# Low weight parts of two stages: ScalarE and an accumulating transfer in place of GpSimd's subtraction

## The chip, the cores and the metric

One core of a Trainium2 chip runs the whole program. The metric is device time in microseconds (us). Five engines run side by side, each with its own queue of instructions in a fixed order: TensorE (PE; its weight loads are PEld), VectorE (DVE), ScalarE (ACT), GpSimd (POOL) and SyncE (SP, which only starts transfers). Transfers that SP starts go through one DMA queue, those that GpSimd starts through another.

## The reference

Two layers over 512 tokens of 1024 columns. What matters here is the first half of a layer: the input projection, the gated channels (u, v) and the output projection `w_o`. All is float32.

```python
h = x @ w_in[i]
q, k, v, qi, ki, wi, u, vs = jnp.split(h, split_points, axis=-1)
a_out = dsa_attention(q, k, v, qi, ki, wi)               # 8 heads, top-k keys
b_out = spatial_gating(gelu(u), gelu(vs), sgu_w[i], ...) # u * (W_s LN(v) + b)
mix = jnp.concatenate([a_out, b_out], axis=-1) @ w_o[i]
x = layer_norm(ALPHA * x + mix, ln1_g[i], ln1_b[i])
```

Behind it stand the feed-forward part and a second layer norm, which the change doesn't touch.

## The kernel before

**Products in three parts.** Each float32 operand is split into a rounded high part h and the rest l = w - h, and a product is three matmuls, h·h, h·l and l·h (`mm3`, L473). For weights `split` (L457) does that: ScalarE casts 1024 columns of the loaded page `raw` into `wh` (L467), and an engine that the caller names subtracts, wl = raw - wh (`low`, L364). The caller names VectorE for all weights but two: for the projection of u (L998) and for the half of `w_o` that the gating feeds (L1021) it is GpSimd, with two subtractions of 512 columns for each split (L468).

**Loops.** `mform` (L482) loads weights in pages of four k-tiles, splits them in pairs of k-tiles, and runs over the four blocks of 128 tokens, each with its own accumulator `acc`, in order "b" (a block through all pairs) or "k" (a pair through all blocks). u has eight k-tiles, so two pages and four splits in a layer; the gating half of `w_o` has four k-tiles for each of two column halves, so two pages and four splits too. There are 8 such splits in a layer, 16 in all.

**Around it.** Before u comes vs: its accumulators are taken by ScalarE (Gelu, `vs`), each block gets a layer norm on VectorE (two `BN_STATS`/`BN_AGGR` steps, a power on GpSimd for `rs`, two SCALAR_TENSOR_TENSOR), ScalarE casts it to `vn` and VectorE takes its low part. All four blocks of vn are needed by the first spatial matmul (`ps<-vn,wsT`, L899), whose result is multiplied with u. Then `w_o`'s gating half runs interleaved with attention (`drive`, L1021).

**Buffers.** `raw` has two pages (L338); `wh` and `wl` have four each (L339); there are four accumulators (L353). A page of `raw` is free for the next load when its last reader is done.

**Order.** Nothing issues in the order of the code. `Order` (L39) records every operation with its operands, and `issue` (L174) plays them through costs written in the code (L136) and hands each engine the sequence that comes out. So a change of an operation moves others on all engines. That sequence is then fixed: an instruction that waits holds all behind it on its engine.

Of the kernel before, what the change touches and what calls it, by code (L numbers as in the profile page):

```python
# [16 lines left out]
OP = mybir.AluOpType  # L17
# [18 lines left out]
RATE_O, RATE_P = 1.4, 1.2  # L36
# [294 lines left out]
def body(ctx: ExitStack, tc: tile.TileContext, x, p, positions, w_in, w_o, ln1_g, ln1_b,  # L331
# [20 lines left out]
    def ACC():  # L352
        return psum.tile([128, 512], F32, name="acc", tag="acc", bufs=4)  # L353
# [10 lines left out]
    def low(eng, dst, src, hi):  # L364
        eng.tensor_tensor(out=dst, in0=src, in1=f32(hi), op=OP.subtract)

    order = Order()
    V, G, A, PE, SY = (order.engine(n, e) for n, e in (
        ("DVE", nc.vector), ("POOL", nc.gpsimd), ("ACT", nc.scalar), ("PE", nc.tensor), ("DMA", nc.sync)))
# [4 lines left out]
    def Xb(b):  # L374
        return X[b // 2][:, b % 2, :]
# [75 lines left out]
    def raw(parts, name="raw"):  # L451
        t = rawp.tile([128, 2048], F32, name="raw", tag="raw")
        for view, src in parts(t):
            SY.dma_start(view, src)
        return t

    def split(src, shape, eng):  # L457

        n = 1
        for s in shape:  # L460
            n *= s
        h = wsp.tile([128, 1024], FR, name="wh", tag="wh")[:, :n]
        l = wsp.tile([128, 1024], FR, name="wl", tag="wl")[:, :n]
        if len(shape) == 2:
            h = h.rearrange("p (a b) -> p a b", b=shape[1])
            l = l.rearrange("p (a b) -> p a b", b=shape[1])
        A.copy(h, src)  # L467
        m = shape[0] // 2 if eng is G else shape[0]  # L468
        for i in range(0, shape[0], m):
            low(eng, l[:, i:i + m], src[:, i:i + m], h[:, i:i + m])  # L470
        return h, l

    def mm3(acc, a, b, start, stop):  # L473

        PE.matmul(acc, a[0], b[0], start=start, stop=False)
        PE.matmul(acc, a[0], b[1], start=False, stop=False)
        PE.matmul(acc, a[1], b[0], start=False, stop=stop)

    def wrows(w, r0, nkt, c0, c1):
        return w[r0:r0 + nkt * 128, c0:c1].rearrange("(k p) n -> p k n", p=128)  # L480

    def mform(xt, kts, load, ncols, order, evac, eng, c0=None, subs=None):  # L482


        ready = subs is not None
        subs = subs or []

        def fetch(i):
            if ready:
                return  # L490
            ks = kts[4 * i:4 * i + 4]
            rv = load(ks)
            for j in range(0, len(ks), 2):
                kk = ks[j:j + 2]
                subs.append((kk, split(rv[:, j:j + len(kk), :], [len(kk), ncols], eng)))

        nf = (len(kts) + 3) // 4

        def piece(b, acc, si):
            kk, (h, l) = subs[si]  # L500
            o = c0(b) if c0 else 0
            for j, k in enumerate(kk):
                mm3(acc[:, o:ncols], xt(k, b), (h[:, j, o:], l[:, j, o:]),
                    k == kts[0], k == kts[-1])

        if order == "k":
            accs = None
            done = 0
            for i in range(nf):
                fetch(i)  # L510
                if accs is None:
                    accs = [ACC() for _ in range(NB)]
                while done < len(subs):
                    for b in range(NB):
                        piece(b, accs[b], done)
                        if subs[done][0][-1] == kts[-1]:
                            evac(b, accs[b])
                        yield
                    done += 1
        else:  # L520
            for i in range(nf):
                fetch(i)
            for b in range(NB):
                acc = ACC()
                for si in range(len(subs)):
                    piece(b, acc, si)
                    if si == len(subs) - 1:
                        evac(b, acc)
                    yield

    def prefetch(load, kts, ncols, eng):
        subs = []
        for i in range(0, len(kts), 4):
            ks = kts[i:i + 4]
            rv = load(ks)
            for j in range(0, len(ks), 2):
                kk = ks[j:j + 2]
                subs.append((kk, split(rv[:, j:j + len(kk), :], [len(kk), ncols], eng)))
        return subs

    def drive(main, *sides):

        have = [-w * r for _, r, w in sides]
        for _ in main:
            for i, (g, rate, _) in enumerate(sides):
                have[i] += rate
                while have[i] >= 1:
                    have[i] -= 1
                    next(g, None)

    def finish(g):
        for _ in g:
            pass

    def mload(w, c0, c1):
        def load(ks):
            n = len(ks)
            t = raw(lambda t: [(t[:, :n * (c1 - c0)].rearrange("p (k n) -> p k n", k=n),
                                wrows(w, ks[0] * 128, n, c0, c1))])
            return t[:, :n * (c1 - c0)].rearrange("p (k n) -> p k n", k=n)  # L560
        return load
# [123 lines left out]
    K8 = list(range(8))  # L685
# [38 lines left out]
    XT = Rows("xt")  # L724
    subs_a = split_a(raws, [V, V, V, V])

    for ly in range(DEPTH):
        wi_l, wo_l, wf_l, wfo_l = w_in[ly], w_o[ly], w_ffn_in[ly], w_ffn_out[ly]
# [71 lines left out]
        def c0(b):  # L800
            return 0 if b else 256

        if ly == 0:
            accs = [ACC() for _ in range(NB)]
            for half in range(2):
                for e in range(2):
                    kk, (h, l) = next(subs_a)
                    for b in range(NB):
                        if e == 0:
                            transpose_rows(XT, b, Xb(b), [half])  # L810
                        for j, k in enumerate(kk):
                            mm3(accs[b][:, c0(b):NA], XT(k, b), (h[:, j, c0(b):], l[:, j, c0(b):]),
                                k == 0, k == 7)
                        if k == 7:
                            evac_a(b, accs[b])
        else:
            finish(mform(XT, K8, None, NA, "b", evac_a, None, c0=c0, subs=subs_a))
# [10 lines left out]
        def evac_q(b, acc):  # L828
# [3 lines left out]
            for half in range(2):  # L832
# [5 lines left out]
                for i in range(4):  # L838
                    PE.transpose(ps[:, i * 128:(i + 1) * 128], sq[:, i], identr)
                A.copy(qT[half][:, :, b * 128:(b + 1) * 128], f32(ps).rearrange("p (k t) -> p k t", k=4))  # L840

        finish(mform(XT, K8, mload(wi_l, 0, 512), 512, "k", evac_q, V))


        vr = raw(lambda t: [(t[:, :1024].rearrange("p (k n) -> p k n", k=8),
                             wrows(wi_l, 0, 8, 640, 768))])
        vh, vl = split(vr[:, :1024].rearrange("p (k n) -> p k n", k=8), [8, 128], V)
        acc = ACC()
        for k in range(8):
# [22 lines left out]
        def evac_vs(b, acc):  # L872
# [4 lines left out]
            low(V, vn[1][:, b], vs, vn[0][:, b])  # L877

        finish(mform(XT, K8, mload(wi_l, 1604, 2116), 512, "k", evac_vs, V))


# [32 lines left out]
        MT = Rows("mt", [])  # L914
# [80 lines left out]
        sp = spatial()  # L995
        MT.more(1)
        finish(sp)
        finish(mform(XT, K8, mload(wi_l, 1092, 1604), 512, "b", evac_u, G))  # L998
        MT.more(0)
        att = attention([0, 1, 2, 3])  # L1000

        def load_o(n0):
            def load(ks):
                def parts(t):
                    v = t.rearrange("p (k n) -> p k n", k=4)
                    cs = slice(n0 * 512, (n0 + 1) * 512)
                    if ks[0] >= 4:
                        return [(v, wrows(wo_l, 512, 4, n0 * 512, (n0 + 1) * 512))]
                    return [(v[g * 64:(g + 1) * 64],
                             wo_l[g * 256:(g + 1) * 256, cs].rearrange("(r d) n -> d r n", d=64))  # L1010
                            for g in range(2)]
                return raw(parts).rearrange("p (k n) -> p k n", k=4)
            return load

        for n in range(2):
            cs = slice(n * 512, (n + 1) * 512)

            def evac_ob(b, acc, cs=cs):
                V.scalar_tensor_tensor(Xb(b)[:, cs], Xb(b)[:, cs], ALPHA, acc, op0=OP.mult, op1=OP.add)

            drive(mform(MT, [4, 5, 6, 7], load_o(n), 512, "k" if n else "b", evac_ob, G), (att, RATE_O, 0))  # L1021

        pr = raw(lambda t: [(t[:, :1024].rearrange("p (b c) -> p b c", b=NB),
                             p[ly, 0].rearrange("(b t) c -> t b c", t=128))])
# [40 lines left out]
        for n in range(2):  # L1065
            cs = slice(n * 512, (n + 1) * 512)
# [135 lines left out]
        if ly < DEPTH - 1:  # L1202
            subs_a = list(split_a([load_a(ly + 1, i) for i in range(2)], [V] * 4))
            XT = Rows("xt")
# [26 lines left out]
```

## Time and profile before

| | us |
|---|---|
| median of 3 runs | 1206.3 (1205.36 to 1207.64) |
| the profiled execution | 1206.69 |
| its span, first to last instruction | 1205.0 |
| TensorE busy in it | 1181.0 |
| VectorE, ScalarE, GpSimd busy | 911.2, 594.1, 154.4 |
| granted TensorE clock, mean | 0.995 |

The span is cut into stretches, and for each the profile gives the busy time of every engine. TensorE's busy time close to a stretch's length means that nothing else can shorten it; what is missing is idle time, and the timeline names for each gap the engine that ended it. The stages that the change touches lie at about 85 to 200 us (layer 0) and 675 to 790 us (layer 1).

### The profile page before, as it was taken

Reading aid. Unit: us, or ns where it says so; the run is one execution under the profiler, and the core shown is the slowest. Engines: PE = TensorE matmul, PEld = TensorE weight load, DVE = VectorE, ACT = ScalarE, POOL = GpSimd, SP = SyncE. Lnnn points to the kernel's source line nnn. Section 1 sums busy time; section 2 is a strip of 40 time slices with the busy share of each in tenths; the row PEclk is TensorE's granted clock in tenths of the full one; section 3 lists DMA queues with packets and bytes.
Section 4 is the critical chain, followed back from the end, with each engine's and each line's share of the span. In section 5 each row is a group of like instructions: output and inputs, shape, how many; then the busy total and the mean of one; then the engine's idle time right before and its main releaser. Section 6 shows DMA issues by size and latency. Waiting matters only on the chain. (4 is left out here: it accounts for less than half of the span.)

```text
span 1205.0 us, 18516 instructions
## 1 busy us (share of the span) xinstructions
PE 1181.0 (98%) x7326; PEld 1053.9 (87%) x7326; DVE 911.2 (76%) x1612; ACT 594.1 (49%) x978; POOL 154.4 (13%) x126
## 2 busy tenths in 40 slices
PE   8999999999999999999999999999999999999997
PEld 7877878789989998989888878778899899899995
DVE  6799998968755755757788999887777477566667
ACT  5545785545633533525345458934465245244340
POOL 0005312110100100000010261121010000000001
PEclk8999999999999999999999999999999999999999
DMA  7232143187871862743511321524685656648141
GB/s 219 71 98 78 36 88 140 36 192 206 183 199 60 188 198 70 208 108 98 192 53 36 121 73 36 140 70 159 150 197 144 173 125 173 175 106 209 53 141 70
DMA packets 124903, 152.76 MB, mean 127 GB/s; under 512 B 6544, under 2 KB 94608, under 8 KB 124816
## 3 DMA queue, kind: packets, MB, share of 16 engines
q1 hardware_dynamic: 101584, 128.51, 33.4%
q0 software_dynamic: 23232, 23.07, 12.5%
q8 instruction: 57, 0.93, 0.3%
q14 instruction: 30, 0.25, 0.1%
HBM read 149.47 MB, written 2.10 MB: 126 GB/s over the span
## 5 line engine op out<-in xcount | busy, mean ns | idle before, releaser
L276 DVE TENSOR_TENSOR wl<-raw,wh 128x1024 fp32r<-128x1024 f32 x178 | 217.3, 1223 | 126.6 <-ACT wh L276 125.7
L276 ACT CAST wh<-raw 128x1024 fp32r<-128x1024 f32 x194 | 203.4, 1050 | 211.1 <-PE acc L276 138.8
L276 PE MATMUL acc<-x1s,wh 128*128 128x256 f32 x1408 | 254.7, 283 | 2.3 <-ACT fg L276 2.3
L276 PEld LDWEIGHTS acc<-x1s,wh 128*128 128x128 f32 x1408 | 219.6, 192 | 2.7 <-ACT fg L276 2.7
L276 PE MATMUL acc<-wh,HT 128*128 128x512 f32 x704 | 218.5, 389 | 0.1
L276 PE MATMUL acc<-x1s,wl 128*128 128x256 f32 x704 | 199.2, 283 | 0.0
L276 PE MATMUL acc<-x1q,wh 128*128 128x256 f32 x1056 | 191.3, 283 | 0.0
L276 PEld LDWEIGHTS acc<-x1q,wh 128*128 128x128 f32 x1056 | 165.2, 192 | 0.6
L276 PEld LDWEIGHTS acc<-wh,HT 128*128 128x128 f32 x704 | 132.1, 188 | 27.6 <-issue 0.5
L276 PE MATMUL acc<-x1q,wl 128*128 128x256 f32 x528 | 149.4, 283 | 0.0
L276 DVE TENSOR_TENSOR wl<-tt,wh 128x1024 fp32r<-128x1024 f32 x66 | 80.8, 1224 | 76.3 <-ACT wh L276 76.2
L276 PE MATMUL acc<-wl,HT 128*128 128x512 f32 x352 | 137.1, 389 | 0.0
L276 PEld LDWEIGHTS acc<-x1s,wl 128*128 128x128 f32 x704 | 135.2, 192 | 0.0
L276 ACT CAST wh<-tt 128x1024 fp32r<-128x1024 f32 x66 | 69.3, 1050 | 130.4 <-PE acc L276 69.3
L276 POOL DMA_DIRECT2D tt<-in_w_ffn_in x44 | 56.4, 1303 | 527.8 <-DMA tt<-in_w_ffn_in 394.2
L276 PEld LDWEIGHTS acc<-x1q,wl 128*128 128x128 f32 x528 | 101.3, 192 | 0.0
L276 PE MATMUL acc<-wh,x1q 128*128 128x512 f32 x256 | 80.2, 392 | 1.4 <-DVE x1q L276 1.0
L276 PEld LDWEIGHTS acc<-wl,HT 128*128 128x128 f32 x352 | 66.1, 188 | 13.5
L276 PE MATMUL acc<-wl,xth 128*128 128x512 f32 x192 | 75.4, 395 | 1.5 <-DVE wl L276 1.5
L276 PE MATMUL acc<-wh,xtl 128*128 128x512 f32 x192 | 75.0, 393 | 0.0
L276 PE MATMUL acc<-wh,xth 128*128 128x512 f32 x192 | 74.9, 396 | 0.1
L276 ACT COPY fg<-acc 128x512 f32<-128x512 f32 x66 | 38.7, 586 | 65.0 <-PE acc L276 65.0
(214 smaller groups left out, 2024.6 us busy)
## 6 DMA issues: line engine op xcount, KB each, us to landing
raw<-in_w_ffn_in SPq DMA_DIRECT2D x22, 1024.0 KB, 5.3
tt<-in_w_ffn_in SPq DMA_DIRECT2D x44, 512.0 KB, 6.0
tt<-in_w_ffn_in POOLq DMA_DIRECT2D x44, 512.0 KB, 7.0
raw<-in_w_ffn_out SPq DMA_DIRECT2D x16, 1024.0 KB, 5.2
raw<-in_w_in SPq DMA_DIRECT2D x12, 1024.0 KB, 5.4
raw<-in_w_ffn_in SPq DMA_DIRECT2D x22, 512.0 KB, 3.6
raw<-in_w_ple_gate SPq DMA_DIRECT2D x8, 1024.0 KB, 5.1
raw<-in_w_ffn_out SPq DMA_DIRECT2D x12, 512.0 KB, 3.8
```

Source lines behind the costliest of these rows:

```text
L276: o.ins = o.fn(*o.a, **o.k)
```

## The change

For u and for the gating half of `w_o`, ScalarE writes -h into the low part right after the cast, and a transfer of GpSimd's queue adds the weights from DRAM onto it. The subtraction on GpSimd is gone, and `raw` is read by the cast alone. Each of the 16 splits loses two GpSimd instructions and gets one on ScalarE and one transfer of 512 KB.

```diff
-    def split(src, shape, eng):
+    def split(src, shape, eng, far=None):
...
         A.copy(h, src)
+        if far is not None:
+            A.mul(l, h, -1.0)
+            G.dma_start(l, far, accum_op=OP.add)
+            return h, l
...
-                subs.append((kk, split(rv[:, j:j + len(kk), :], [len(kk), ncols], eng)))
+                f = far(kk) if far else None
+                subs.append((kk, split(rv[:, j:j + len(kk), :], [len(kk), ncols], eng, f)))
...
-        finish(mform(XT, K8, mload(wi_l, 1092, 1604), 512, "b", evac_u, G))
+        finish(mform(XT, K8, mload(wi_l, 1092, 1604), 512, "b", evac_u, G,
+                     far=lambda ks: wrows(wi_l, ks[0] * 128, len(ks), 1092, 1604)))
...
-            drive(mform(MT, [4, 5, 6, 7], load_o(n), 512, "k" if n else "b", evac_ob, G), (att, RATE_O, 0))
+            drive(mform(MT, [4, 5, 6, 7], load_o(n), 512, "k" if n else "b", evac_ob, G,
+                        far=lambda ks, cs=cs: wo_l[512 + (ks[0] - 4) * 128:512 + (ks[-1] - 3) * 128, cs]
+                        .rearrange("(k p) n -> p k n", p=128)), (att, RATE_O, 0))
```

The sequences move with it. In layer 0 the weights of u are wh/wl 342/343, 344/345, 347/348 and 349/350, the accumulators of vs are 305 to 308 and those of u 351, 354, 357, 360. ScalarE at the start of u:

```order
 L276 CAST wh_342<-raw_341 128x1024
+L276 ACTIVATE wl_343<-wh_342 128x1024
 L276 CAST wh_344<-raw_341 128x1024
 L276 ACT_TABLE_LOAD
 L276 ACTIVATE vs_314<-acc_305 128x512
 L276 ACTIVATE vs_318<-acc_306 128x512
+L276 ACTIVATE vs_322<-acc_307 128x512
+L276 ACTIVATE wl_345<-wh_344 128x1024
+L276 ACTIVATE vs_326<-acc_308 128x512
 L276 CAST wh_347<-raw_346 128x1024
```

One new ACTIVATE stands ahead of the table load, one ahead of the evacuation of the last vs block. TensorE at the start of u, before:

```order
L276 MATMUL acc_351<-wh_342,xth_106 128x512 [waits Activation_49]
L276 MATMUL acc_351<-wl_343,xth_106 128x512 [waits Pool_49]
L276 MATMUL acc_351<-wh_342,xtl_107 128x512
L276 MATMUL acc_351<-wh_342,xth_106 128x512
L276 MATMUL acc_351<-wl_343,xth_106 128x512 [waits Pool_49]
```

and now:

```order
L276 MATMUL acc_351<-wh_342,xth_106 128x512 [waits Activation_49]
L276 MATMUL acc_354<-wh_342,xth_106 128x512 [waits Activation_49]
L276 MATMUL acc_357<-wh_342,xth_106 128x512 [waits Activation_49]
L276 MATMUL acc_360<-wh_342,xth_106 128x512 [waits Activation_49]
L276 MATMUL acc_351<-wl_343,xth_106 128x512 [waits DMASW0_49]
```

All four accumulators are now opened ahead of the first low part. TensorE where the spatial matmuls begin, before (65 matmuls of u stand ahead of the first row here):

```order
L276 MATMUL acc_357<-wh_347,xtl_109 128x512
L276 MATMUL ps_337<-vn_298,wsT_331 128x256 [waits PE_49,Activation_49]
L276 MATMUL ps_338<-vn_298,wsT_331 128x256 [waits DVE_49]
L276 MATMUL acc_357<-wh_349,xth_108 128x512
L276 MATMUL acc_357<-wl_350,xth_108 128x512
```

and now (36 matmuls of u ahead of the first row here):

```order
L276 MATMUL acc_354<-wh_344,xth_106 128x512
L276 MATMUL ps_337<-vn_298,wsT_331 128x256 [waits PE_49,Activation_49]
L276 MATMUL ps_338<-vn_298,wsT_331 128x256 [waits DVE_49]
L276 MATMUL ps_339<-vn_298,wsT_331 128x256 [waits DVE_49]
L276 MATMUL acc_354<-wl_345,xth_106 128x512
L276 MATMUL acc_354<-wh_344,xtl_107 128x512
```

The first spatial matmul stands behind 37 matmuls of u in place of 66; in layer 1 it is 38 in place of 61. GpSimd's queue through the same stretch of layer 0:

```order
-L276 TENSOR_TENSOR wl_343<-raw_341,wh_342 128x512 x2
-L276 TENSOR_TENSOR wl_345<-raw_341,wh_344 128x512 x2
-L276 TENSOR_TENSOR wl_348<-raw_346,wh_347 128x512
+L276 DMA wl_343<-in_w_in 128x2x512
 L276 TENSOR_TENSOR rs_317<-rs_317,mhalf_78 128x1
 L276 TENSOR_TENSOR rs_321<-rs_321,mhalf_78 128x1
-L276 TENSOR_TENSOR wl_348<-raw_346,wh_347 128x512
-L276 TENSOR_TENSOR wl_350<-raw_346,wh_349 128x512 x2
+L276 DMA wl_345<-in_w_in 128x2x512
+L276 DMA wl_348<-in_w_in 128x2x512
```

The second transfer stands behind the powers of the first two layer-norm blocks.

## Rows read from the trace of the kernel before

**Rows 1.** The page's busy times: engine, us, share of the span, instructions.

```profile
PE 1181.0 (98%) x7326; PEld 1053.9 (87%) x7326; DVE 911.2 (76%) x1612; ACT 594.1 (49%) x978; POOL 154.4 (13%) x126
```

**Rows 2.** Stretches: length, busy PE, PEld, DVE, ACT, POOL, clock, DMA share, GB/s.

```profile
75.00:100.00 25.00, 23.47 (x114) 19.36 (x113) 24.51 (x65) 10.63 (x16) 9.70 (x9) 1.00 0.37 127
100.00:125.00 25.00, 24.02 (x123) 19.77 (x122) 24.53 (x49) 13.01 (x23) 12.19 (x10) 1.00 0.16 50
150.00:175.00 25.00, 23.63 (x131) 18.58 (x130) 23.45 (x67) 21.95 (x53) 3.87 (x3) 1.00 0.38 82
...
700.00:725.00 25.00, 24.54 (x134) 20.20 (x133) 23.97 (x66) 17.16 (x37) 11.55 (x9) 1.00 0.25 82
...
750.00:775.00 25.00, 23.72 (x137) 19.63 (x136) 20.38 (x50) 23.16 (x49) 3.32 (x3) 1.00 0.59 141
```

**Rows 3.** TensorE's timeline: start, length, engine, operation, [idle before, and who ended it].

```profile
85.11 0.50 PE L276 MATMUL acc<-wl,xth 128*128 128x512 f32 x1 [1.53 <-DVE wl L276]
...
119.26 0.63 PE L276 MATMUL ps<-ident,u 128*128 128x128 f32 x4 [0.98 <-ACT wh L276]
```

**Rows 4.** TensorE's timeline: two matmuls in a row, first spatial matmuls of both layers.

```profile
99.11 0.39 PE L276 MATMUL acc<-wl,xth 128*128 128x512 f32 x1
99.34 0.39 PE L276 MATMUL acc<-wh,xtl 128*128 128x512 f32 x1
...
110.22 0.47 PE L276 MATMUL ps<-vn,wsT 128*128 128x256 f32 x2
...
702.43 0.40 PE L276 MATMUL ps<-vn,wsT 128*128 128x256 f32 x2
```

**Rows 5.** ScalarE's timeline at the start of u, layer 0 and layer 1.

```profile
89.16 2.01 ACT L276 CAST wh<-raw 128x1024 fp32r<-128x1024 f32 x2 [11.68 <-DMA raw<-in_w_in]
91.19 1.28 ACT L276 ACT_TABLE_LOAD   x1
92.48 1.09 ACT L276 ACTIVATE vs<-acc 128x512 f32<-128x512 f32 x2
...
109.50 0.62 ACT L276 CAST vn<-vs 128x512 fp32r<-128x512 f32 x1 [1.42 <-DVE vs L276]
...
680.91 2.00 ACT L276 CAST wh<-raw 128x1024 fp32r<-128x1024 f32 x2 [12.98 <-DMA raw<-in_w_in]
```

**Rows 6.** ScalarE's groups by form: shapes, count, busy us, mean ns, idle before.

```profile
L276 ACT ACTIVATE fg<-fg 128x512 f32<-128x512 f32 x22 | 13.8, 628 | 0.0
...
L276 ACT ACTIVATE P<-P,rc 128x512 f32<-128x512 f32 x8 | 5.8, 730 | 0.0
```

**Rows 7.** GpSimd's group by form that the change removes.

```profile
L276 POOL TENSOR_TENSOR wl<-raw,wh 128x512 fp32r<-128x512 f32 x32 | 44.4, 1419 | 61.7 <-ACT wh L276 61.7
```

**Rows 8.** VectorE's timeline in the layer norm of vs, layer 0 and layer 1.

```profile
101.73 1.78 DVE L276 SCALAR_TENSOR_TENSOR vs<-vs,rs,sg_b 128x512 f32<-128x512 f32 x1
...
108.72 0.75 DVE L276 SCALAR_TENSOR_TENSOR vs<-vs,rs,sg_b 128x512 f32<-128x512 f32 x1
...
686.24 1.28 DVE L276 BATCH_NORM_STATS2 st<-vs 128x6 f32<-128x512 f32 x2
...
693.67 1.63 DVE L276 SCALAR_TENSOR_TENSOR vs<-vs,mv,sg_g 128x512 f32<-128x512 f32 x1
...
702.71 0.68 DVE L276 TENSOR_TENSOR vn<-vs,vn 128x512 fp32r<-128x512 f32 x1
```

**Rows 9.** DMA issues at 301, at 252, all loads: count, KB each, us to landing.

```profile
tt<-in_w_ffn_in POOLq DMA_DIRECT2D x1, 512.0 KB, 5.8
...
tt<-in_w_ffn_in POOLq DMA_DIRECT2D x2, 512.0 KB, 11.0
...
raw<-in_w_in SPq DMA_DIRECT2D x12, 1024.0 KB, 5.4
```

**Rows 10.** SyncE's timeline: the second load of u's weights, layer 1.

```profile
687.17 0.38 SPq L276 DMA_DIRECT2D raw<-in_w_in  x1
```

More of the change, by code (lines that the diff above doesn't have):

```diff
@@ L480, in wrows, with mform @@
         return w[r0:r0 + nkt * 128, c0:c1].rearrange("(k p) n -> p k n", p=128)
-    def mform(xt, kts, load, ncols, order, evac, eng, c0=None, subs=None):
+    def mform(xt, kts, load, ncols, order, evac, eng, c0=None, subs=None, far=None):
         ready = subs is not None
```

## The prediction, made before the changed kernel had run

> **What bounds the kernel now.** The page's busy line comes first: TensorE is busy 1181.0 us [rows 1] of a span of 1205.0, so only 24 us of the span can be saved by anything but fewer matmuls, and the change leaves every matmul in place. The stretches come next [rows 2]: where the change works, TensorE is busy 23.47, 24.02, 23.63, 24.54 and 23.72 us out of 25, at a granted clock of 1.00. VectorE is as full there (24.51, 24.53, 23.45, 23.97), except in the last; ScalarE and GpSimd are not. So an edit here either fills those idle microseconds or adds to them.
>
> The gap of 1.53 us at 85.11 [rows 3] is ended by VectorE before u's weights have arrived, and the change can't touch it. It is all the idle time of the first stretch. The other four have 0.98 (one gap, ended by ScalarE [rows 3]), 1.37, 0.46 and 1.28: **4.1 us in all, which is the most that can be won**.
>
> **What it removes.** 32 subtractions on GpSimd, 1419 ns each, 44.4 us [rows 7]. GpSimd is busy 13% and no gap in [rows 3] is ended by it: direct worth 0. An indirect worth is larger. A layer-norm instruction on VectorE takes 1.78 us while GpSimd subtracts and 0.75 us when it doesn't [rows 8]: 1.03 us more, for four of them in each layer, so VectorE gets back some **4.1 us a layer**, just in the chain that spatial gating waits for. And `raw` is read by the cast alone: in layer 1 the second load of u stands at 687.17 [rows 10], held by GpSimd's reading; it can go when both casts are done, at 680.91 + 2.00 [rows 5] plus the 1.05 of a new ACTIVATE between them, 684.0, about 3 us earlier.
>
> **What it adds on ScalarE.** One ACTIVATE of 128x1024 per split. No such row exists. Rows of 512 columns take 628 and 730 ns [rows 6]; a cast takes 0.62 at 512 columns [rows 5] and 1.00 in steps of two (2.01 for two), so 512 more columns cost 0.4 to 0.43. Bounds 1.05 and 1.16; I take 1.05, since the row with one input is the nearer, with a step of 1.0 between neighbours. Eight in a layer make 8.4 us on an engine with 12 us idle in each of the first two stretches, but with 3 and 2 us idle in 150-175 and 750-775 [rows 2].
>
> **What it adds as transfers.** One of 512 KB per split, in GpSimd's queue. The kernel has the same kind: 5.8 us from issue to landing for one alone, 11.0 for the median of two issued together [rows 9]. Those are the bounds; I take 5.8 for the first, and little more for the others, since GpSimd's queue gets them one by one as ScalarE finishes. So a low part that came 1.4 to 2.8 us after its cast now comes 1.05 + 5.8 = 6.9 us after it, and the order covers that by opening all four accumulators first.
>
> **Layer 0, instruction by instruction.** Matmuls follow each other at 0.2275 us ([rows 4]: 0.23 between neighbours), so 66 of them before the first spatial matmul at 110.22 [rows 4] say that u began at about 95.2.
> - ScalarE's first cast begins at 89.16; a new ACTIVATE stands between the two casts, so the table load moves from 91.19 to 92.2 and the first evacuation from 92.48 to 93.5 [rows 5]. The accumulators of vs come free a microsecond later; the fourth stands behind another ACTIVATE, ready about 97.0. TensorE opens three accumulators, then waits: **1.2 us idle**.
> - The first low part: cast and ACTIVATE end at 91.3, landing 97.1, just covered by that. The second transfer goes out at 97.4, behind two powers, and lands at 103.2: 24 matmuls end at 102.7, **0.5 us idle**. Nine more end at 105.2.
> - Then the spatial matmuls, which want the last layer-norm block. From the first statistics to the end of the chain layer 1 shows 686.24 to 703.39 (702.71 plus 0.68) [rows 8], 17.1 us; less 4.1 it is 13.0. It begins with the end of the first evacuation, 93.5 plus 0.63 [rows 6], 94.15; that ends it at 107.2, with a half microsecond for new ACTIVATEs ahead of the last cast on ScalarE: 107.7. **2.4 us idle.**
>
> Before, 66 matmuls were done when spatial began at 110.22; now 37 are done at 107.7. The 29 that are still to do cost 29 x 0.2275 = 6.6 us, and the start is 2.5 us earlier: layer 0 leaves this point **4.1 us late**. (The three gaps sum to 4.1.) The vector work is faster; the order has been packed as if the layer norm were ready at once, and the cover of 29 matmuls that hid it is behind it.
>
> **Layer 1.** 38 matmuls ahead in place of 61, 23 x 0.2275 = 5.2 us. The chain starts as in layer 0 5.0 us after the first cast, 680.91 [rows 5], at 685.9, and 13.0 later with 1.2 for ScalarE it is 700.1; before, spatial began at 702.43 [rows 4], so 2.3 earlier: **2.9 us late**, all of it as idle time before the first spatial matmul.
>
> **Softmax and `w_o`.** The four ACTIVATEs of `w_o` stand on ScalarE ahead of the first exponentials and of the transposes of u. The idle 0.98 before 119.26, already ended by ScalarE [rows 3], becomes about 1.5; in layer 1 the 0.46 of 700-725 becomes about 1: **+0.5 each, +1.0**. Less after that: 1.37 and 1.28 us are idle in 150-175 and 750-775 [rows 2], where ScalarE is busy 21.95 and 23.16; work that entered 3 to 4 us later on TensorE finds these two engines further ahead, and about half of the idle time closes: **-1.3**.
>
> Sum: 4.1 + 2.9 + 1.0 - 1.3 = **+6.7 us**. On the profiled execution's 1206.69 that is 1213.4; the median of the three runs lies 0.4 lower, so **1213.0**.
>
> **The rivals.** *A, the other side: VectorE's relief decides.* VectorE has 24.5 of 25 us busy at the start of u; 8.2 us come back over both layers. If the last block of the layer norm is ready at 105.2 in place of 107.7, the wait before spatial falls away, and the earlier attention work fills the 4.1 us of idle time. It decides if the chain takes 10.5 us or less. For it: four slow rows, and u's multiplies are relieved too. Against it: 13.0 already counts all four at 0.75. It gives from 1206.3 - 4.1 = 1202.2, all idle time won, to 1208.7, with 2.4 us of waits left over. Chance 0.22.
>
> *B: the transfers land late.* If neighbours in GpSimd's queue cost 11.0 and not 5.8 [rows 9], the second low part of layer 0 lands at 108.4. Ahead of it 24 matmuls are done at 102.7, so TensorE waits 5.7, the nine matmuls end at 110.5, and spatial then waits for nothing: 110.5 in place of 107.7, +2.8. In layer 1 the second transfer goes out at about 687.7, lands at 698.7 and has 14 matmuls behind it, 3.2 us: 701.9 in place of 700.1, +1.8. It gives 1213.0 + 4.6 = 1217.6. For it: 11.0 is a row of this kernel, and u's transfers go out about 2 us apart. Against it: SP's queue is nearly idle at 100-125 (DMA share 0.16 [rows 2]). Chance 0.16.
>
> A mechanism of the same kind in layer 1: u's second page, issued some 3 us earlier, now travels beside two accumulating transfers; if they share evenly, a page that lands in 5.4 alone [rows 9] lands up to half of 5.8, 2.9 us, later, and layer 1 loses what the earlier issue gave: 1213.0 + 2.9 = 1215.9. That is inside the range, and 0.04 of B's chance is its. The Trainium skill states that rule in DMA: Bandwidth & Descriptors, section SWDGE vs HWDGE vs iDMA: inside each DMA engine software and hardware queues feed different internal queues, and the engine takes them in turn. The trace of before has no row here of a load of SP beside one of GpSimd's by itself, so it neither agrees nor disagrees.
>
> *C: the change does nothing that shows.* Were the ACTIVATEs and the landings hidden under the idle times above, the time would be 1206.3. This is the middle of A and is counted there.
>
> **How the numbers follow.** The forecast's case has 0.62 and reaches from 1208.7 (the waits at u's start half as long) to 1217 (ACTIVATE at 1.16, and a microsecond more in each of the two waits for spatial). About 0.2%, 2.4 us, is what a measurement of this kernel can tell from no change. Faster than 1203.9 is only the lower third of A, 0.08; within 0.2% the rest of A, 0.14; slower is the forecast and B, 0.78. The range runs from 1205.5, which leaves out half of A (0.11), to 1218.5, which leaves out the upper part of B (0.06).
>
> **What would show it.** A group of 16 ACTIVATEs near 1.05 us and of 16 transfers landing near 5.8. VectorE's layer-norm rows at 0.75 throughout. TensorE's gaps before acc<-wl of 0.5 and before ps<-vn of 2 to 3 us, the latter ended by ScalarE's cast of vn, in both layers; 5 to 7 us idle in 75-125 in place of 2.5; some 31 us idle in the whole span in place of 24. The forecast is wrong if spatial starts in layer 0 without a gap (A), if the gap is ended by a transfer (B), or if the waits ahead of the first softmax are gone.

## The result, and the profile after

The changed kernel takes 1213.9 us (median of 4 runs, 1212.29 to 1214.23) against 1205.83 for the kernel before: a ratio of 1.0066, 95% interval 1.0053 to 1.0079, **8 us slower**. The forecast was 6.7 us slower. The profiled execution has a span of 1212.0.

The busy line answers to [rows 1]: engine, us, share of the span, instructions.

```profile
PE 1181.5 (97%) x7326; PEld 1054.4 (87%) x7326; DVE 903.4 (75%) x1612; ACT 607.7 (50%) x994; POOL 129.8 (11%) x110
```

TensorE is 0.5 us busier in a span that is 7.0 us longer, so nearly all of the loss shows as idle time. (Matmuls that ran slower in layer 0 are inside the busy time; what they cost is read from the timeline below.) GpSimd lost 24.6 us of work, VectorE 7.8.

The stretches answer to [rows 2]: length, busy PE, PEld, DVE, ACT, POOL, granted clock, DMA share, GB/s.

```profile
75.00:100.00 25.00, 19.04 (x85) 15.07 (x85) 24.21 (x68) 13.38 (x20) 5.71 (x6) 0.94 0.59 162
100.00:125.00 25.00, 24.42 (x113) 19.74 (x112) 21.05 (x52) 9.83 (x19) 4.41 (x4) 0.92 0.53 111
150.00:175.00 25.00, 24.63 (x145) 20.78 (x144) 23.66 (x68) 23.35 (x57) 4.66 (x3) 1.00 0.50 108
...
675.00:700.00 25.00, 22.17 (x102) 18.08 (x101) 21.45 (x57) 11.11 (x15) 4.54 (x6) 1.00 0.60 157
700.00:725.00 25.00, 22.66 (x116) 18.33 (x115) 23.87 (x55) 15.22 (x26) 5.62 (x6) 1.00 0.59 131
...
750.00:775.00 25.00, 24.89 (x149) 21.17 (x147) 21.94 (x65) 23.82 (x58) 3.87 (x3) 1.00 0.43 85
```

Three things are new. TensorE is idle 6 us of 75-100 and 2.8 and 2.3 us at the start of u in layer 1. The clock is at 0.94 and 0.92 in layer 0, where it was 1.00. And the DMA share at 100-125 is 0.53, where it was 0.16. In return 150-175 and 750-775 have 0.4 and 0.1 us idle, where they had 1.37 and 1.28.

TensorE's timeline of the changed kernel names the gaps (start, length, engine, operation, [idle before, and who ended it]); it answers to [rows 3] and [rows 4].

```profile
94.80 0.50 PE L276 MATMUL acc<-wh,xth 128*128 128x512 f32 x1 [0.41 <-ACT vs L276]
99.32 0.80 PE L276 MATMUL acc<-wl,xth 128*128 128x512 f32 x1 [4.02 <-DMA wl<-in_w_in]
99.92 0.63 PE L276 MATMUL acc<-wh,xtl 128*128 128x512 f32 x1
100.34 0.63 PE L276 MATMUL acc<-wh,xth 128*128 128x512 f32 x1
...
104.10 0.40 PE L276 MATMUL acc<-wh,xth 128*128 128x512 f32 x1
104.33 0.40 PE L276 MATMUL acc<-wl,xth 128*128 128x512 f32 x1
109.76 0.61 PE L276 MATMUL ps<-vn,wsT 128*128 128x256 f32 x3 [0.48 <-ACT vn L276]
...
695.91 0.50 PE L276 MATMUL acc<-wl,xth 128*128 128x512 f32 x1 [2.83 <-DMA wl<-in_w_in]
706.10 0.50 PE L276 MATMUL ps<-vn,wsT 128*128 128x256 f32 x2 [2.15 <-ACT vn L276]
```

The two long gaps before acc<-wl are ended by a transfer of u's low part. Behind the first, starts lie 0.42 us apart (99.92 to 100.34) where they lay 0.23 apart: the lower of the clock's two levels, 1.2 GHz, until 104.10. Eleven matmuls took 4.8 us in place of 2.5, 2.3 us that no idle row shows.

Why the transfers came late stands in the DMA issues of two short stretches, about 90 (layer 0) and about 687 (layer 1): operation, count, KB each, us to landing. They answer to [rows 9].

```profile
raw<-in_w_o SPq DMA_DIRECT2D x1, 1024.0 KB, 6.7
wl<-in_w_in POOLq DMA_DIRECT2D x1, 512.0 KB, 9.5
...
raw<-in_w_in SPq DMA_DIRECT2D x1, 1024.0 KB, 8.3
wl<-in_w_in POOLq DMA_DIRECT2D x1, 512.0 KB, 8.7
```

The first transfer took 9.5 and 8.7 us, not 5.8, and each time a load of 1 MB on SP's queue began within a microsecond of it. Those loads are the work of the change itself: `raw` is free once the cast has read it, so SyncE starts the next page at once, in layer 0 the first page of `w_o`, in layer 1 u's second page (8.3 us in place of 5.4).

ScalarE's timeline shows who held vn in both layers; the rows answer to [rows 5].

```profile
88.42 1.06 ACT L276 ACTIVATE wl<-wh 128x1024 fp32r<-128x1024 f32 x1
...
107.06 1.05 ACT L276 CAST wh<-raw 128x1024 fp32r<-128x1024 f32 x1 [4.55 <-PE acc L276]
108.14 1.06 ACT L276 ACTIVATE wl<-wh 128x1024 fp32r<-128x1024 f32 x1
109.11 0.60 ACT L276 CAST vn<-vs 128x512 fp32r<-128x512 f32 x1
...
696.23 1.05 ACT L276 CAST wh<-raw 128x1024 fp32r<-128x1024 f32 x1 [4.10 <-DMA raw<-in_w_in]
697.18 0.61 ACT L276 CAST vn<-vs 128x512 fp32r<-128x512 f32 x1
...
705.43 0.62 ACT L276 CAST vn<-vs 128x512 fp32r<-128x512 f32 x1 [1.00 <-DVE vs L276]
```

The new ACTIVATE takes 1.06. In layer 0 the last vn cast stood at 109.11 behind a cast of `w_o` that waited 4.55 us for a `wh` buffer which TensorE still read. VectorE's last multiply of the layer norm was long done there. In layer 1 it is otherwise: the first vn cast stood behind the cast of u's late second page, VectorE waited 2.52 us for it, and so the last vn cast had to wait for VectorE. VectorE's timeline in both layers (answers to [rows 8]):

```profile
92.46 1.27 DVE L276 BATCH_NORM_STATS2 st<-vs 128x6 f32<-128x512 f32 x2
...
103.15 0.75 DVE L276 SCALAR_TENSOR_TENSOR vs<-vs,mv,sg_g 128x512 f32<-128x512 f32 x1
104.41 0.75 DVE L276 SCALAR_TENSOR_TENSOR vs<-vs,rs,sg_b 128x512 f32<-128x512 f32 x1
...
697.83 0.69 DVE L276 TENSOR_TENSOR vn<-vs,vn 128x512 fp32r<-128x512 f32 x1 [2.52 <-ACT vn L276]
...
704.64 0.75 DVE L276 SCALAR_TENSOR_TENSOR vs<-vs,rs,sg_b 128x512 f32<-128x512 f32 x1 [0.44 <-POOL rs L276]
```

The kernel before began that chain in layer 0 with this row, and its last multiply ended at 109.47 [rows 8]:

```profile
94.18 1.28 DVE L276 BATCH_NORM_STATS2 st<-vs 128x6 f32<-128x512 f32 x2
```

So VectorE's relief is real: every such row is at 0.75, and in layer 0 the chain, from the first statistics to the end of the last multiply, took 12.7 us (92.46 to 105.16) in place of 15.3. It bought nothing there, since the cast behind it came 4 us later. In layer 1 the chain took 15.2 us (690.16 to 705.39) against 15.4 before: the wait for the first vn cast used up nearly all that the faster rows gave.

**By stage.** Executions are up to 2.4 us apart before u is reached (the transposes ahead of spatial start at 82.55 before and 80.87 after), so the stages are measured from there: from those transposes to the first matmul of the gate after the layer norm (acc<-x1q,wh: at 261.65 before and 265.00 now; in layer 1 from 687.27 to 853.15 before, from 691.12 to 860.48 now). Layer 0 is 5.0 us longer, layer 1 3.5. The same measure for every kernel that was run, one execution each (e1's is the longest of its four):

| kernel | median us | ratio to before, interval | layer 0 | layer 1 |
|---|---|---|---|---|
| the change | 1213.9 | 1.0066 (1.0053 to 1.0079) | +5.0 | +3.5 |
| e1, only u | 1214.8 | 1.0078 (1.0061 to 1.0095) | +4.5 | +7.3 |
| e2, only w_o | 1214.6 | 1.0075 (1.0060 to 1.0090) | +2.5 | +6.0 |
| e3, w_o pages a quarter | 1210.3 | 1.0040 (1.0025 to 1.0055) | +1.6 | +3.4 |
| e4, vn cast on VectorE | 1212.7 | 1.0062 (1.0046 to 1.0079) | +5.0 | +2.9 |
| e5, u's second page too | 1206.6 | 1.0012 (1.0003 to 1.0021) | +1.4 | 0.0 |
| e6, GpSimd adds | 1212.1 | 1.0060 (1.0045 to 1.0075) | +0.7 | +6.5 |
| e7, second pages of both | 1204.0 | 0.9992 (0.9983 to 1.0001) | +0.4 | -0.3 |
| e8, u's second page | 1201.7 | 0.9969 (0.9959 to 0.9980) | -2.7 | -1.5 |
| e9, u but its first split | 1205.1 | 0.9997 (0.9988 to 1.0007) | -2.1 | +1.4 |
| e10, w_o's second half | 1203.9 | 0.9990 (0.9980 to 0.9999) | -1.2 | +0.4 |

### The profile page after: what moved, and what is told of

It is laid out like the page before. It is cut to its first block, busy times and chain, and to the rows that moved or that the text cites. A ratio compares the mean times of both kernels' runs of the same rounds, so it can differ in the third digit from the quotient of the medians.

```text
span 1212.0 us, 18519 instructions
## 1 busy us (share of the span) xinstructions
PE 1181.5 (97%) x7326; PEld 1054.4 (87%) x7326; DVE 903.4 (75%) x1612; ACT 607.7 (50%) x994; POOL 129.8 (11%) x110
```

## The experiments

**Which half loses (e1, e2).** The theory after the first look at the trace: the loss is made at the start of u.

```diff
-            drive(mform(MT, [4, 5, 6, 7], load_o(n), 512, "k" if n else "b", evac_ob, G, far=...), ...)
+            drive(mform(MT, [4, 5, 6, 7], load_o(n), 512, "k" if n else "b", evac_ob, G), ...)
```

> Only u's weights get -hi and the transfer; the gating half of w_o goes back to two GpSimd subtractions per split. Theory (the loss is made at the start of u: the first transfers land 9 us after issue, TensorE idles and drops its clock): nearly the whole loss stays, +6 to +9 us on the kernel before, about 1213. Rival (the ACTIVATEs of w_o ahead of the first softmax cost as much): +3 to +4 us, about 1209.5.

1214.8, 9.4 us slower than before and so a little over the theory's +6 to +9, with the gaps of the change in both layers (3.98 and 2.75 us, ended by the transfer). The four executions lie in two pairs, at 1213.2 and at 1216.4 and 1216.8; the trace is of the longest, so the +7.3 of layer 1 in the table is the upper pair's. And the other half alone:

```diff
-        finish(mform(XT, K8, mload(wi_l, 1092, 1604), 512, "b", evac_u, G, far=...))
+        finish(mform(XT, K8, mload(wi_l, 1092, 1604), 512, "b", evac_u, G))
```

> Only the gating half of w_o gets -hi and the transfer; u goes back to GpSimd. Theory (loss at the start of u): within 1 us of the kernel before, 1205 to 1207, with the clock at full speed at the start of u. Rival (w_o's ACTIVATEs ahead of the softmax): +3 to +4 us, about 1209.5.

1214.6: the theory missed, and so did its rival in size. Alone, `w_o` loses about as much as u, most of it at its own start (a gap of 0.92 us at 695.74, ended by a cast of u's second page, lies earlier). TensorE's timeline of e2 there, layer 0 and layer 1:

```profile
122.15 0.50 PE L276 MATMUL acc<-wh,mth 128*128 128x512 f32 x1 [0.68 <-ACT mth L276]
124.35 0.63 PE L276 MATMUL ps<-ident,u 128*128 128x128 f32 x4 [1.70 <-DVE u L276]
125.66 0.80 PE L276 MATMUL acc<-wh,mth 128*128 128x512 f32 x1
126.25 0.63 PE L276 MATMUL acc<-wl,mth 128*128 128x512 f32 x1
...
719.72 0.63 PE L276 MATMUL ps<-ident,u 128*128 128x128 f32 x4 [1.51 <-DVE u L276]
723.51 0.48 PE L276 MATMUL ps<-ident,P 128*128 128x128 f32 x1 [1.82 <-ACT P L276]
```

With the first low part far off, the order puts four h·h matmuls (one before the change) and transposes ahead that TensorE runs out of: waits of 0.7 to 1.8 us, and again matmuls of 0.63 us at the lower clock behind them. No transfer ends these gaps; that the order makes them is read from the rows, and e10 below, which leaves the first half of `w_o` alone, has in layer 0 only the gap of about 1 us that the kernel before has too [rows 3]. The two halves don't add up: 9.4 and 9.1 alone, 8 together. In the change the first transfer of `w_o` lands at 115.4, while u's matmuls run to 127.8, and one h·h matmul stands ahead of the first low part; in e2 it lands at 124.6, 4.9 us after u's last matmul began.

**Why the transfers are late (e3, e5).** The order of instructions is the change's own (in e5 a few rows on ScalarE, VectorE and GpSimd trade places in layer 1), and only the bytes of SP's loads shrink.

```diff
-                        return [(v, wrows(wo_l, 512, 4, n0 * 512, (n0 + 1) * 512))]
+                        return [(v[:, :1], wrows(wo_l, 512, 1, n0 * 512, (n0 + 1) * 512))]
...
-                return raw(parts).rearrange("p (k n) -> p k n", k=4)
+                t = raw(parts).rearrange("p (k n) -> p k n", k=4)
+                return t[:, :1].to_broadcast([128, 4, 512]) if ks[0] >= 4 else t
```

> The changed kernel in the same order of instructions, but the loads of w_o's gating half bring one k-tile of four (256 KB in place of 1 MB; the cast reads that tile four times, the transfers are whole). The output of w_o's gating half is therefore another. Theory (u's first transfers share the DMA engines with the w_o pages, which start early because raw is free after the cast): the first landing in layer 0 goes from 9 to about 6 us, the 4.0 us gap to about 1, no half-speed matmuls behind it, and 3.5 to 5 us of the loss go: 1209 to 1210.5. Rival (a transfer started while GpSimd's queue was idle takes 9 us by itself): gap and time stay, 1213 to 1214.

1210.3, 3.6 us less than the change by the medians, all of it in layer 0 of the traces. The issues about 90, the transfer issued at 96.88, and TensorE's rows:

```profile
raw<-in_w_o SPq DMA_DIRECT2D x1, 256.0 KB, 3.7
wl<-in_w_in POOLq DMA_DIRECT2D x1, 512.0 KB, 7.0
...
wl<-in_w_in POOLq DMA_DIRECT2D x1, 512.0 KB, 8.4
```

```profile
96.68 0.64 PE L276 MATMUL acc<-wl,xth 128*128 128x512 f32 x1 [1.56 <-DMA wl<-in_w_in]
97.12 0.63 PE L276 MATMUL acc<-wh,xtl 128*128 128x512 f32 x1
```

A quarter of the neighbour's bytes takes 2.5 us off the same transfer (9.5 to 7.0) and off the gap (4.02 to 1.56). One thing was expected and didn't come: the clock fell all the same, for some eight matmuls. And bytes of the page are not all: u's third transfer, issued 1.3 us behind the second in GpSimd's own queue, still took 8.4 us (8.8 in the change), though the page beside it was a quarter too; no gap of TensorE hangs on it.

e5 does the same to u's second page (`quarter` is the old loader, but brings one k-tile of the second page):

```diff
-        finish(mform(XT, K8, mload(wi_l, 1092, 1604), 512, "b", evac_u, G,
+        finish(mform(XT, K8, quarter, 512, "b", evac_u, G,
```

> As e3_quarter_pages, and u's second page of weights too is loaded as one k-tile of four (read four times by the casts; u's output is another, the transfers are whole). Theory (in layer 1 u's first transfer and its second page go out within a microsecond and take each other's bandwidth, and the late page holds the cast of vn behind it on ScalarE): the 2.75 us gap before acc<-wl falls below 1.2 and the 2.13 us gap before spatial below 1.2; 2.5 to 3.5 us less than e3_quarter_pages, about 1207. Rival (a transfer takes that long by itself): as e3_quarter_pages, 1210 to 1211.

1206.6, 3.8 us less than e3 and 1.5 more than before. Layer 1, TensorE's gaps and the issues about 683.5:

```profile
689.90 0.50 PE L276 MATMUL acc<-wl,xth 128*128 128x512 f32 x1 [0.19 <-DMA wl<-in_w_in]
698.85 0.50 PE L276 MATMUL ps<-vn,wsT 128*128 128x256 f32 x2 [0.90 <-ACT vn L276]
```

```profile
wl<-in_w_in POOLq DMA_DIRECT2D x1, 512.0 KB, 6.6
raw<-in_w_in SPq DMA_DIRECT2D x1, 256.0 KB, 3.1
```

Both gaps of layer 1 go together (2.83 and 2.15 in the change, 0.19 and 0.90 here): the transfer lands after 6.6 us, and the page no longer holds the vn cast. The change is 8.1 us slower than before and e5 1.5, so 6.6 us of the loss go with the bytes of two loads (7.3 between the two medians). That those bytes lengthen the transfer is shown; a kernel that keeps the loads whole and starts them later was not run.

**ScalarE's queue (e4).**

```diff
-            A.copy(vn[0][:, b], vs)
+            V.tensor_copy(vn[0][:, b], vs)
```

> The changed kernel with the four casts of vn on VectorE in place of ScalarE. Theory (ScalarE's queue holds the last casts of vn behind the cast of a page that waits for its load or its buffer): the 2.15 us gap before spatial in layer 1 goes, the 0.48 of layer 0 too, -2 to -2.7 us on the changed kernel, about 1211.5; the gaps ended by a transfer stay at 4.0 and 2.8. Rival (the layer norm's own chain on VectorE is late): four more instructions on VectorE make it longer, 1214 to 1215.5.

1212.7; against the change the time is not told apart (the intervals overlap). In the trace the 0.48 of layer 0 is gone and the 2.15 of layer 1 is 1.16, now ended by VectorE. But the order moved too: 43 and 49 matmuls of u stand ahead of spatial in place of 37 and 38, so these are not the same waits, and e4 does not price ScalarE's queue. It shows another one behind it: in layer 1 VectorE now waits 2.85 us for a power on GpSimd (at 703.06), which stands behind a transfer that waits for its ACTIVATE.

**Is it the ACTIVATE? (e6).**

```diff
-            G.dma_start(l, far, accum_op=OP.add)
+            for i in range(2):
+                G.tensor_tensor(out=l[:, i:i + 1], in0=f32(l[:, i:i + 1]), in1=src[:, i:i + 1], op=OP.add)
```

> ScalarE writes -hi as in the change, but GpSimd adds raw onto it in two instructions per split in place of the transfer. Theory (the transfer's landing is the loss, the ACTIVATE is not): 1205 to 1207.5. Rival (the ACTIVATEs ahead of the evacuations and casts are the loss): 1210 to 1212.

1212.1 is the rival's number, but not for its reason. Layer 0, with all eight ACTIVATEs, loses 0.7 us. So the ACTIVATEs cost little there. The rest is layer 1, in SyncE's and TensorE's rows:

```profile
690.89 0.38 SPq L276 DMA_DIRECT2D raw<-in_w_in  x1
```

```profile
697.40 0.73 PE L276 MATMUL acc<-wh,xth 128*128 128x512 f32 x2 [3.47 <-ACT wh L276]
```

The addition stands 1 us behind the cast and behind two powers, so `raw` is held 3.7 us longer than before (690.89 against 687.17 [rows 10]), the second page comes late, and TensorE runs out of u's first page; some eight matmuls from 698.2 on then run at the lower clock as well. Here `raw` came free too late; in the change it came free early and its load got in the way.

**Where a transfer has cover (e7 to e10).** u's first page alone is 48 matmuls over the four blocks, 48 x 0.2275 = 10.9 us, more than the 5.9 to 9.5 us in which u's transfers landed in the change.

```diff
+                     far=lambda ks: wrows(wi_l, ks[0] * 128, len(ks), 1092, 1604) if ks[0] >= 4 else None))
```

> Only u's second page (splits 3 and 4) gets -hi and the transfer; all else as before. Theory (covered by the 48 matmuls of the first page): 1204 to 1206.5, and the layer norm of vs has two or more of its slow rows back at 0.75. Rival (the transfers disturb the layer norm's casts on ScalarE and the order): +2 to +4 us, 1207.5 to 1209.5.

1201.7, **0.31% faster than the kernel before** (0.20 to 0.41%), and faster than was expected. VectorE's timeline in layer 0, and two stretches:

```profile
96.11 0.75 DVE L276 SCALAR_TENSOR_TENSOR vs<-vs,rs,sg_b 128x512 f32<-128x512 f32 x1 [0.38 <-POOL rs L276]
...
104.14 0.75 DVE L276 SCALAR_TENSOR_TENSOR vs<-vs,rs,sg_b 128x512 f32<-128x512 f32 x1
```

```profile
100.00:125.00 25.00, 25.00 (x131) 20.70 (x130) 24.35 (x56) 12.80 (x22) 10.23 (x9) 1.00 0.39 90
...
150.00:175.00 25.00, 24.88 (x145) 20.84 (x144) 23.16 (x65) 23.10 (x54) 3.86 (x3) 1.00 0.49 106
```

The two transfers of layer 0 land 9.2 us after issue here too (median), but no gap there is ended by one, and in layer 1 a single one of 0.39. All layer-norm rows are at 0.75, and TensorE is busy through 100-125. This looks like rival A of the prediction with half of u's transfers; but no run separates VectorE's relief from the other things that moved with the order, so what the gain comes from is not shown.

With `w_o`'s second half as well (e7; n is the column half):

```diff
-                        far=lambda ks, cs=cs: wo_l[512 + ...
+                        far=None if n == 0 else lambda ks, cs=cs: wo_l[512 + ...
```

> The change only where other matmuls of the same product stand ahead: u's second page (splits 3 and 4) and the second column half of w_o; the first page of u and the first half of w_o keep GpSimd's subtraction. Theory (a transfer costs only where its low part is the first that is wanted): 1204 to 1207, no gap above 1 us that is ended by a transfer. Rival (every transfer costs, some 0.5 us each): 1209 to 1210.

1204.0, gaps of 1.20 (over the 1 us expected) and 0.52 ended by a transfer: level with before, and 2.3 us behind e8. The 1.20 is before a low part of u's second page, whose transfer took 10.4 us here and 9.1 in e8, so the 48 matmuls are a thin cover. The second half of `w_o` alone (e10):

> Only the second column half of w_o gets -hi and the transfer. Theory (its low parts are wanted 48 matmuls and the attention between later): no gap that is ended by a transfer; what remains are ScalarE's four ACTIVATEs in a stretch where it is busy 22 of 25 us: 1204.5 to 1208. Rival (as e2_wo_only, any transfer of w_o costs): 1209 to 1212.

1203.9, just under the range: no gap ended by a transfer, and 0.1% faster than before, with an interval (0.01 to 0.20%) that ends close to no change. Last, u without its first split (e9):

```diff
+                     far=lambda ks: wrows(wi_l, ks[0] * 128, len(ks), 1092, 1604) if ks[0] >= 2 else None))
```

> As e8_u_second_page, but the second split of u's first page too gets -hi and the transfer: only the first keeps GpSimd's subtraction. Theory (cover decides: the first split gives 24 matmuls over four blocks, 5.5 us, against a landing some 8 us after u begins): gaps of 2 to 3 us ended by a transfer in each layer, 1204 to 1208, worse than e8_u_second_page. Rival (what e8 gained is VectorE's relief, which grows with every subtraction that goes): 1199.5 to 1201.

1205.1, 3.4 us behind e8, as the theory expected and its rival did not. But the reason is shown only in part: the gaps ended by a transfer are 0.71 in layer 0 and 0.31 and 0.70 in layer 1, not 2 to 3; the larger part of layer 1's loss lies later, a gap of 1.57 at 749.48 ended by the softmax on ScalarE, and what moved that was not tried.

## Why the prediction was right, and where its steps were not

**The time** held: 1213.0 forecast, 1213.9 measured, +6.7 against +8.

**The ceiling, the ACTIVATE, VectorE.** The first two held. No kernel's median won more than the 4.1 us of idle time; e8, the best, won 3.4. The ACTIVATE is 1.06 us (1.05 forecast), and the slow layer-norm rows are back at 0.75. The chain is another matter: 4.1 us a layer were to come back, and 2.6 did in layer 0 (15.3 to 12.7) and 0.1 in layer 1. The forecast's 13.0 us also ran to the end of the last low part, which the first spatial matmul doesn't wait for (before, it started at 110.22 [rows 4], right after the last cast at 109.50 [rows 5]); to that same end the chain took 18.0 us in layer 0 and 17.0 in layer 1. The earlier load in layer 1 came true too, at some 687.9 with the kernel 3.85 us late at that point, and it was half of the harm.

**The transfer, 5.8 us.** This term was mis-sized, and it is the main one: 9.5 in layer 0, 8.7 in layer 1, a median of 8.8 over u's eight. Rival B had the right effect, a late landing, and for the first transfer of each layer, on which the long gaps hang, the wrong neighbour: not GpSimd's own queue but SP's loads. (A transfer close behind another of its own queue is late too: 8.4 us in e3.) What the prediction set against it, SP's queue being nearly idle at 100-125 (0.16 [rows 2]), was read from a stretch that the change itself fills, since it frees `raw`. For layer 1 the mechanism was seen and given 0.04. Page and transfer lengthen each other there: the page from 5.4 to 8.3 us and the transfer, by e5, from 6.6 to 8.7. The Trainium skill states (DMA: Bandwidth & Descriptors, section SWDGE vs HWDGE vs iDMA) that software and hardware queues feed different internal queues of each DMA engine, which it serves in turn. The lengthening agrees with that; the taking of turns stands in no row here.

**Layer 0, instruction by instruction.** The gaps were forecast as 1.2 + 0.5 + 2.4 = 4.1, and came as 0.41 + 4.02 + 0.48 = 4.9, with the clock's 2.3 on top, which was not foreseen. The count of 29 matmuls held: u began at 93.54 and spatial at 109.76, 16.2 us with 37 matmuls done, where 66 took 15.0; 6.6 + 1.2 = 7.8 us late at this point, against 4.1.

**Layer 1.** 2.9 was forecast, all before spatial. It came as 2.83 before the first low part and 2.15 before spatial, u from 691.91 to 706.10: 14.2 us for 38 matmuls where 61 took 14.4 (688.06 to 702.43), 5.2 - 0.2 = 5.0 us late.

**What comes back.** Forecast were +1.0 at the softmax and -1.3 after it. Of the 7.8 and 5.0, 2.8 and 1.5 came back by the end of the stage, 4.3 us where the two terms together gave 0.3. In 150-175 and 750-775 the idle time closed by 1.0 and 1.2 us, the way that was described, and the waits ahead of the first softmax did not grow by half a microsecond each: in layer 0 the 0.98 is gone and 0.48 stands at 134.25, in layer 1 it is 0.55 at 730.01. The rest of what came back was not foreseen. So two errors of about 6 and 4 us, the start too cheap and the recovery too small, nearly cancelled. That the total is better than its parts is luck.

**The cause of the wait before spatial.** Forecast as the layer norm's chain on VectorE, ended by ScalarE's cast. It was ended by that cast in both layers. In layer 0 VectorE had been done for 4 us and ScalarE's queue held the cast; in layer 1 the cast did wait for VectorE, which the late page had held up. So of the signs that the forecast named, the ACTIVATE, the layer-norm rows, the idle time in 75-125 (6.5 us) and in the whole span (30.5 us) held; the landing near 5.8 and the 2 to 3 us before spatial in layer 0 did not, and the long gap there is one that a transfer ended.

Not settled: why a given gap loses the clock and another doesn't (below), and what part of the recovery, or of e8's gain, is VectorE's relief.

## What to carry to other kernels

A buffer that comes free earlier starts the next load earlier: look at what that load will now run beside, before taking a landing time from a quiet stretch. A low part made by a longer path belongs where other work of the same product already stands ahead (u's second page, e8), not where TensorE waits for it first. Halves of a change need not add up; time them apart before deciding which of them to keep.

## What the runs showed of the hardware

Transfers of both queues lengthen each other by their bytes: a 512 KB accumulating transfer landed after 7.0 us beside a load of 256 KB (e3) and after 9.5 beside one of 1 MB (the change).

In these runs the clock's fall does not follow from the length of a gap. After gaps of 4.02 (the change, layer 0), 3.47 (e6, layer 1), 2.75 (e1, layer 1) and 1.56 us (e3, layer 0) matmuls ran at 1.2 GHz; after 2.83 (the change, layer 1), 1.53 [rows 3] and 1.36 (e5, layer 0) they kept 2.4 GHz. Ahead of each gap TensorE's timeline has no wait of over 0.6 us for at least 11 us. The stretches of e1 (first) and of the change (second) beside their gaps, columns as above:

```profile
694.00:696.00 2.00, 1.11 (x3) 0.92 (x4) 0.41 (x1) 0.90 (x1) 0.00 (x0) 0.62 1.07 293
696.00:698.00 2.00, 2.00 (x7) 1.57 (x6) 1.30 (x3) 2.00 (x5) 0.07 (x1) 0.53 1.10 262
```

```profile
694.00:696.00 2.00, 0.09 (x1) 0.10 (x1) 1.31 (x3) 0.00 (x0) 0.00 (x0) 1.00 1.08 295
696.00:698.00 2.00, 2.00 (x9) 1.63 (x10) 0.17 (x1) 1.77 (x3) 0.00 (x0) 1.00 1.10 262
```

The same gap, a clock of 0.53 in one and 1.00 in the other, 1.5 us apart in what they cost (seven matmuls took 3.1 us in e1).
